# The last projection of a two-layer hybrid backbone: its sixteen row tiles inside the attention's pools

## The chip, the cores and the metric

The kernel runs on one core of a Trainium2 chip. The metric is the device time of one execution in microseconds (us). A core has a matrix engine (TensorE, PE in the profile), whose weight loads have a row of their own (PEld), and VectorE (DVE), ScalarE (ACT) and GpSimd (POOL). SyncE (SP) issues most of the DMAs; each engine takes its instructions in the order of its own queue.

## The reference, cut to what matters

Two layers run over 2048 latent tokens of width 1024 with 256 context tokens ahead of them. The second, odd layer is a neighbourhood attention with 16 heads of 64. Its end is all that the change touches:

```
def odd_mixer(h, hc, w_in, q_gain, k_gain, rpb, w_out, update_ctx):
    ...
    o = neighborhood_attention(q_x, k_x, v_x, k_c, v_c, rpb)
    y = jnp.dot(o.reshape(h.shape[0], h.shape[1], C_WIDTH) * jax.nn.silu(z_x), w_out)
    ...
x = x + gate * y
```

So for each block of 128 tokens (a row tile) the attention's output is multiplied by its gate path, then by a 1024 x 1024 weight, then by a gate vector, and added to the residual stream.

## The kernel before

**Numbers.** All values are float32. A product of matrices is made from two halves of each operand, a rounded high part and the remainder, in the type float32r: high by high, high by low, low by high, three matmuls for each slice of 128 in the sum (L129 to L131 in `mm3_steps`). One row tile of the projection is two halves of 512 columns by eight slices by three, 48 matmuls of 128 x 512.

**The attention.** `odd_attention` (L1306) goes over eight pairs of heads (j) and, in each, over twenty steps: four of context keys and sixteen blocks of 128 latent keys, n = 0 to 15. A step makes scores on TensorE (L1373, L1374), adds a table to them on VectorE (L1535), takes exp on ScalarE, and four to six steps later `flush` multiplies the result by the values (L1406) and adds it to running sums on GpSimd (L1412). For each block of 512 query tokens (bb = 0 to 3) `finish_block` divides by the sums (L838 to L845) and stores the result in a DRAM scratch RT1 from GpSimd's queue (L848). For the last pair the blocks are finished after n = 7, 11 and 15 (two at once).

**The tag "opt".** `exps` (L1322) hands out tiles of 4 KB a partition from a pool with eleven buffers of one tag. The exps of the attention live there, and so do the raw slices of the output weight (L1443), which is loaded and split in the last pair of heads while the attention still runs. The two halves of the weight go into buffers that the attention no longer needs (old query tiles, a value tile, tables, context keys).

**The end.** Row tile 0 is made ready inside the last steps: z0 (gate path) and r0 (attention's output) are loaded and multiplied (L1549 to L1551), x0 (residual) and the gate vector are loaded, and hi0 and lo0 are split (L1558); these are five tiles of "opt". After the last step z1, r1 and x1 of row tile 1 are loaded (L1564 to L1568; x1 in the place of the mask). Then come 6 triples of matmuls of tile 0, the rest of the attention (`flush(4)`), the rest of tile 0, the product r1 times z1 on GpSimd (L1579), the last `flush(0)`, the split of r1 (L1584, into the place of the running sums "oacc0"), and tile 1's matmuls.

**The separate stage.** `odd_attention` then closes the pools that it opened itself, and `odd_tail` (L1589) opens three new ones (wpA, wpS on chip, wpP in PSUM) and calls `project` for row tiles 2 to 15 (L1598). `project` (L1080) loads z, r and x of a tile (`project_load`, L1045), multiplies r by z on GpSimd (L1056), splits (`project_split`, L1059: high part on ScalarE, remainder on VectorE at L1061), and runs `project_steps` (L1063): 48 matmuls, after each 24 the gate on VectorE (L1072) and the residual on GpSimd (L1073), then the store of the tile from SP's queue (L1074). Every tag there has two buffers (four PSUM banks).

**Order of the work.** The program is traced as written; a planner then simulates it and puts every engine's queue in order, so that an instruction may be moved ahead of others whose inputs come later. Three things bind it: a tile's buffer has to be free, `issue_after` puts what is traced behind a named instruction of the same engine, and `load` (L108) chains the loads of the attention on SP's queue in the order of the text. The loads of `project_load` have no such chain.

Of the kernel before, what the change touches and what calls it, by code (L numbers as in the profile page):

```python
# [11 lines left out]
F32R = mybir.dt.float32r  # L12
AF = mybir.ActivationFunctionType
ALU = mybir.AluOpType
AX = mybir.AxisListType
PSUM = bass.MemoryType.PSUM

P = 128
D = 1024
KD = D // P  # L20
SEQ = 2048
CTX = 256
T = SEQ + CTX
NT = T // P
NCT = CTX // P
# [63 lines left out]
class Kern:  # L89
# [1216 lines left out]
    def odd_attention(self, out, right, left, wout):  # L1306

        nc = self.nc
        self.RT1 = self.scr("RT1", (KD, P, SEQ), F32)
        NR, NC = (len(b) for b in BLOCKS["k"])  # L1310
        with ExitStack() as es:
            self.ln_exp(self.last_tanh, es)
            kcp, vp, qa, qb, kp, tp, lp = right
            ap, rp, fp, ep = [self.pool(es, "oa" + n, bufs=2, side="left", reuse_waits="tile") for n in "KRFP"]
            pp = self.pool(es, "oaP", bufs=2, space=PSUM, reuse_waits="tile")
# [5 lines left out]
            bank = lambda: self.tl(pp, [P, 512], "st", bufs=4)  # L1321
            exps = lambda shape=[P, 2, 512], dt=F32: self.tl(ep, shape, "opt", dt, bufs=11)  # L1322
# [132 lines left out]
            def rows(tile, RT, o, ks):  # L1455
                self.load(tile[:, ks, :], RT[ks, :, o * P : o * P + P].rearrange("j p t -> p j t"))
# [15 lines left out]
            all_k, most_k = slice(0, KD), slice(0, KD - 1)  # L1472
# [18 lines left out]
            for j in range(8):  # L1491
                OA[j] = {}, {}
                for s, (kind, n) in enumerate(steps):
                    g, c = divmod(n, 4)
# [19 lines left out]
                    for i in range(2):  # L1514
# [17 lines left out]
                        for ro, ri, rn in pieces("k", 0, g, r0_, nr):  # L1532
                            for co, ci, cn in pieces("k", 1, c, c0, w):
                                d = slice(ro, ro + rn), slice(co, co + cn)
                                nc.vector.tensor_tensor(out=pt[:, d[0], d[1]], in0=ps[:, d[0], d[1]],  # L1535
                                                        in1=tabs[j][i][:, ri : ri + rn, ci : ci + cn], op=ALU.add)
# [15 lines left out]
                    elif j == 7 and n == 12:  # L1552
                        x0 = exps([P, D])
                        self.load(x0[:], self.x1[CTX : CTX + P, :])
                        gate = ones["kt"][0][:].rearrange("p i c -> p (i c)").bitcast(F32)
                        self.load(gate, self.gates[1, 0:1].partition_broadcast(P))
                        hi0, lo0 = [exps([P, KD, P], F32R) for _ in range(2)]
# [3 lines left out]
                            flush(4)  # L1561
            for _ in out_s:
                pass
            z1, r1 = [exps([P, KD, P]) for _ in range(2)]  # L1564
            rows(z1, self.z1, 1, all_k)
            rows(r1, self.RT1, 1, all_k)
            x1 = self.tl(ap, [P, NR, NC], "maskk", bufs=1)[:].rearrange("p r c -> p (r c)")[:, :D]
            self.load(x1, self.x1[CTX + P : CTX + 2 * P, :])  # L1568
            y = lambda: self.tl(fp, [P, 512], "rc", bufs=3)
            first = self.project_steps(hi0, lo0, x0, gate, wout, bank, y, out[:P, :])  # L1570
            with self.tc.issue_after(mm.ins):
                for _ in range(6):
                    mm = next(first)
# [2 lines left out]
            with self.tc.issue_after(mm.ins):  # L1576
                for mm in first:
                    pass
            nc.gpsimd.tensor_tensor(out=r1[:], in0=r1[:], in1=z1[:], op=ALU.mult)  # L1579
            with self.tc.issue_after(mm.ins):  # L1580
                flush(0)
            parts = self.tl(rp, [P, 2, 16, 64], "oacc0", F32R, bufs=1)
            hi1, lo1 = [parts[:, i].rearrange("p r c -> p (r c)").rearrange("p (k t) -> p k t", k=KD) for i in range(2)]
            self.project_split(r1[:], hi1, lo1)  # L1584
            for _ in self.project_steps(hi1, lo1, x1, gate, wout, bank, y, out[P : 2 * P, :]):
                pass
        return gate

    def odd_tail(self, out):  # L1589
        with ExitStack() as es:  # L1590
            kcp, va, qb0, vb, tb, lp, ta, qa, kp, qb1 = [self.pool(es, "oa" + n, bufs=2, side="right", reuse_waits="tile")
                                                         for n in ("KC", "VA", "QB", "VB", "TB", "L", "TA", "QA", "KT", "QC")]
            left = self.pool(es, "wpX", side="left", reuse_waits="tile")
            w = {}
            gate = self.odd_attention(out, (kcp, (va, vb), qa, (qb0, qb1), kp, (ta, tb), lp), left, w)
            ld, sp = [self.pool(es, n, bufs=2, side="left", reuse_waits="tile") for n in ("wpA", "wpS")]
            pp = self.pool(es, "wpP", bufs=2, space=PSUM, reuse_waits="tile")
            self.project(1, self.RT1, [(t, t - NCT) for t in range(NCT + 2, NT)], self.x1, out, w, sp, pp, ld, {}, [gate], self.z1)  # L1598

    def build(self, es, out):  # L1600
        self.consts(es)
# [95 lines left out]
```

## Time and profile before

| what | value |
|---|---|
| time, median of 3 runs | 3742.54 us (3739.37 to 3745.3) |
| the profiled execution's own time | 3737.21 us |
| span of its profile | 3735.4 us |
| TensorE busy | 3586.5 us, 96% of the span |
| VectorE, ScalarE, GpSimd busy | 2377.3, 1438.4, 1209.3 us |
| mean granted TensorE clock | 0.977 of full speed |

How to read it: the page's times are those of one profiled execution, counted from the start of its span. "PE pj L131" is a matmul of line 131 that writes a tile named pj. In brackets behind an instruction stands how long its engine was idle ahead of it and what ended that. In the table by stretches each engine has its busy time and, after x, its instructions; behind them come the granted clock of TensorE, the share of the DMA engines that was busy and the GB/s. Matmuls overlap: one of 128 x 512 is shown as 0.39 us, while the next starts 0.23 us after it.

### The profile page before, as it was taken

What the parts mean: (1) busy time and instruction counts of PE and PEld (TensorE: products, weight loads), DVE (VectorE), ACT (ScalarE), POOL (GpSimd) and SP (SyncE); (2) the same over time, 40 slices, a digit from 0 to 9 for tenths busy, and PEclk for the clock granted to TensorE, in tenths of its full rate; (3) what the DMA queues carried; (4) which work ended last, traced back from release to release, by engine and by line L of the source; (5) the groups of instructions that cost most, each with busy time, mean ns of one, the idle gap of its engine ahead of it and who ended that gap; (6) DMA issues with size and microseconds to landing.
All of it is one profiled execution on the core that took longest, in us unless ns stands there. A gap on an engine that the chain in (4) does not pass through costs nothing.

```text
span 3735.4 us, 51753 instructions
## 1 busy us (share of the span) xinstructions
PE 3586.5 (96%) x18404; PEld 2766.2 (74%) x18404; DVE 2377.3 (64%) x4860; ACT 1438.4 (39%) x2741; POOL 1209.3 (32%) x1336
## 2 busy tenths in 40 slices
PE   7999989999999999999999999999899999999889
PEld 6988987888886666655657878888688886555567
DVE  4677656888866666697654345545578774566722
ACT  4445541111125555545552134444322224444400
POOL 1434330001011222212202233333444435776643
PEclk9999999999999999999999999999999999999999
DMA  7455452222242241434515545445544438778464
GB/s 258 135 167 160 128 170 95 82 76 85 74 137 66 69 113 58 115 88 136 143 51 169 168 145 152 147 142 169 187 139 135 140 104 228 182 197 206 144 194 129
DMA packets 364371, 512.18 MB, mean 137 GB/s; under 512 B 25825, under 2 KB 243889, under 8 KB 358210
## 3 DMA queue, kind: packets, MB, share of 16 engines
q1 hardware_dynamic: 322642, 425.49, 39.1%
q0 software_dynamic: 19872, 55.92, 5.0%
q10 hardware_dynamic: 21600, 27.46, 2.1%
q8 instruction: 146, 2.39, 0.3%
q14 instruction: 111, 0.91, 0.1%
HBM read 329.38 MB, written 179.37 MB: 136 GB/s over the span
## 4 chain that ended last, share of the span: by engine, by line
PE 78%; DMA 9%; DVE 7%; ACT 2%; POOL 2%; issue 2%; SPq 0%; POOLq 0%; ACTq 0%; DVEq 0%
PE gm L129 9%; PE gm L130 9%; PE gm L131 9%; PE av L905 7%; PE st L963 4%; PE mx L651 4%; PE st L964 3%; PE st L965 3%; PE pj L129 3%; PE pj L130 3%; PE pj L131 3%; DMA kt<-K1t 2%; PE o L1406 2%; PE st L1373 2%; DMA wraw<-w_od 1%
## 5 line engine op out<-in xcount | busy, mean ns | idle before, releaser
L954 DVE TENSOR_TENSOR acc<-acc,apt 128x512 f32<-128x512 f32 x512 | 365.4, 738 | 155.9 <-ACT apt L106 153.0
L106 ACT ACTIVATE apt<-st 128x512 f32<-128x512 f32 (+1 forms) x592 | 344.6, 594 | 284.1 <-PE st L965 250.8
L652 DVE TENSOR_REDUCE mm<-mx 128x1 f32<-128x512 f32 (+1 forms) x656 | 389.2, 629 | 82.0 <-PE mx L651 75.0
L905 PE MATMUL av<-apt,av 128*64 128x512 f32 (+1 forms) x1184 | 287.6, 599 | 0.0
L963 PE MATMUL st<-aq,akh 97*128 97x512 f32 (+1 forms) x592 | 254.0, 429 | 5.1 <-ACT apt L106 2.7
L651 PE MATMUL mx<-mk,mq 96*128 96x512 f32 (+1 forms) x656 | 236.7, 373 | 6.3 <-DMA mq<-QT 4.7
L964 PE MATMUL st<-aq,akh 96*128 96x512 f32 (+1 forms) x592 | 235.3, 398 | 0.0
L965 PE MATMUL st<-aq,akl 96*128 96x512 f32 (+1 forms) x592 | 234.1, 396 | 0.0
L1286 DVE CUSTOM_DVE_ANT_1 mx<-mx,mtab 128x225 f32<-128x225 f32 (+12 forms) x576 | 183.8, 339 | 59.5 <-PE mx L1280 44.2
L1535 DVE TENSOR_TENSOR opt<-st,tab 128x64 f32<-128x64 f32 (+10 forms) x576 | 143.0, 316 | 115.5 <-PE st L1374 90.2
L106 ACT ACTIVATE u<-gm 128x352 f32<-128x352 f32 (+1 forms) x140 | 68.6, 497 | 371.0 <-PE gm L131 208.7
L905 PEld LDWEIGHTS av<-apt,av 128*64 128x64 f32 x1184 | 82.0, 138 | 156.8 <-issue 155.5
L963 PEld LDWEIGHTS st<-aq,akh 97*128 97x128 f32 x592 | 112.3, 190 | 98.0 <-issue 43.7
L1412 POOL TENSOR_TENSOR oacc<-oacc,opt 128x682 f32<-128x682 f32 (+9 forms) x144 | 169.5, 1200 | 28.0 <-ACT opt L106 26.9
L1073 POOL TENSOR_TENSOR px<-py,px 128x512 f32<-128x512 f32 x64 | 86.4, 1350 | 232.2 <-DVE py L1072 229.6
L106 ACT ACTIVATE opt<-opt 128x930 f32<-128x930 f32 (+8 forms) x130 | 104.4, 805 | 123.9 <-DVE opt L1535 115.1
L106 ACT ACTIVATE prh<-pr 128x1024 fp32r<-128x1024 f32 x32 | 33.9, 1058 | 263.0 <-PE pj L130 235.3
L651 PEld LDWEIGHTS mx<-mk,mq 96*128 96x128 f32 x656 | 121.7, 189 | 17.8 <-issue 5.1
L1373 PE MATMUL st<-q,kt 128*128 128x480 f32 (+5 forms) x256 | 104.4, 410 | 31.6 <-DVE opt L1535 15.9
L965 PEld LDWEIGHTS st<-aq,akl 96*128 96x128 f32 x592 | 113.7, 192 | 25.5
L964 PEld LDWEIGHTS st<-aq,akh 96*128 96x128 f32 x592 | 114.0, 193 | 18.1
L106 ACT ACTIVATE x<-px,modB,modA 128x128 f32<-128x128 f32 x272 | 99.3, 469 | 58.0 <-PE px L331 55.3
(517 smaller groups left out, 10097.4 us busy)
## 6 DMA issues: line engine op xcount, KB each, us to landing
q<-Q SPq DMA_DIRECT2D x48, 512.0 KB
H<-x ACTq DMA_DIRECT2D x36, 512.0 KB
adaw<-ada_w SPq DMA_DIRECT2D x64, 256.0 KB
x<-H SPq DMA_DIRECT2D x32, 512.0 KB
pr<-RT SPq DMA_DIRECT2D x32, 512.0 KB
wraw<-w_od SPq DMA_DIRECT2D x64, 256.0 KB
K1t<-okt POOLq DMA_DIRECT2D x32, 512.0 KB, 7.7
kt<-K1t SPq DMA_DIRECT2D x32, 512.0 KB
```

The source lines that it names most:

```text
L106: return self.nc.scalar.activation(out, in_, func, **kw)
L129: self.nc.tensor.matmul(out, lh(k), rh(k), start=j == 0, stop=False)
L130: self.nc.tensor.matmul(out, lh(k), rl(k), start=False, stop=False)
L131: yield self.nc.tensor.matmul(out, ll(k), rh(k), start=False, stop=j == n - 1)
L651: mm = nc.tensor.matmul(ps[:, :w], q[:A_QK, (t % 6) * P : (t % 6) * P + P], k[:A_QK, k0 : k0 + w], start=True, stop=True)
L652: nc.vector.tensor_reduce(out=m[:, t, n : n + 1], in_=ps[:, :w], axis=AX.X, op=ALU.max)
L905: nc.tensor.matmul(O[j, nb][i * 64 : i * 64 + 64, :w], V[j, kt // TT][:, kt % TT, i * 64 : i * 64 + 64], pts[i][:, :w], start=n == 0, stop ...
L954: nc.vector.tensor_tensor(out=acc[i][:, :w], in0=a[:, :w], in1=pts[i][:, :w], op=ALU.add)
L963: nc.tensor.matmul(ps[:, :w], kh[: A_QK + 1, i, kq], qh[: A_QK + 1, :w], start=True, stop=False)
L964: nc.tensor.matmul(ps[:, :w], kh[:A_QK, i, kq], ql[:A_QK, :w], start=False, stop=False)
L965: mm = nc.tensor.matmul(ps[:, :w], kl[:A_QK, i, kq], qh[:A_QK, :w], start=False, stop=True)
L1286: nc.vector.tensor_tensor_reduce(out=s, in0=s, in1=tb[:, ri : ri + rn, ci : ci + cn], scale=1.0, scalar=-3e38, op0=ALU.add, op1=ALU.max, a ...
```

## The change

The stage of `project` and its three pools are gone; `odd_tail` now only calls `odd_attention`, and all sixteen row tiles run in that function's pools. `fetch(o)` takes three tiles of "opt" and loads z, r and x of row tile o through the chained `load`; `ready` multiplies r by z on GpSimd, takes two more tiles of "opt" (five for each row tile; tile 1 keeps "oacc0" for its halves) and splits. Tiles 1 and 2 are fetched ahead of tile 0's matmuls. In the loop, ahead of the matmuls of tile o, tile o + 1 is made ready and tile o + 2 is fetched. x1 is no longer in the mask's place. The product of tile 1 now stands behind the last `flush(0)` in the text. PSUM banks are the attention's tag "st" (four) in place of "pj" (four), and the tiles between VectorE and GpSimd are its tag "rc" (three) in place of "py" (two). `project_steps`, `project_split` and `load` are unchanged.

```diff
-            z1, r1 = [exps([P, KD, P]) for _ in range(2)]
-            rows(z1, self.z1, 1, all_k)
-            rows(r1, self.RT1, 1, all_k)
-            x1 = self.tl(ap, [P, NR, NC], "maskk", bufs=1)[:].rearrange("p r c -> p (r c)")[:, :D]
-            self.load(x1, self.x1[CTX + P : CTX + 2 * P, :])
             y = lambda: self.tl(fp, [P, 512], "rc", bufs=3)
-            first = self.project_steps(hi0, lo0, x0, gate, wout, bank, y, out[:P, :])
+            tok = lambda o: slice(CTX + o * P, CTX + o * P + P)
+
+            def fetch(o):
+                z, r, x = exps([P, KD, P]), exps([P, KD, P]), exps([P, D])
+                rows(z, self.z1, o, all_k)
+                rows(r, self.RT1, o, all_k)
+                self.load(x[:], self.x1[tok(o), :])
+                return z, r, x
+
+            def ready(z, r, x, parts=None):
+                nc.gpsimd.tensor_tensor(out=r[:], in0=r[:], in1=z[:], op=ALU.mult)
+                hi, lo = parts or [exps([P, KD, P], F32R) for _ in range(2)]
+                self.project_split(r[:], hi[:], lo[:])
+                return hi, lo, x
+
+            steps_of = lambda o, hi, lo, x: self.project_steps(hi, lo, x, gate, wout, bank, y, out[o * P : o * P + P, :])
+            first = steps_of(0, hi0, lo0, x0)
+            got = {o: fetch(o) for o in (1, 2)}
             with self.tc.issue_after(mm.ins):
                 for _ in range(6):
                     mm = next(first)
...
-            nc.gpsimd.tensor_tensor(out=r1[:], in0=r1[:], in1=z1[:], op=ALU.mult)
             with self.tc.issue_after(mm.ins):
                 flush(0)
             parts = self.tl(rp, [P, 2, 16, 64], "oacc0", F32R, bufs=1)
...
-            self.project_split(r1[:], hi1, lo1)
-            for _ in self.project_steps(hi1, lo1, x1, gate, wout, bank, y, out[P : 2 * P, :]):
-                pass
-        return gate
+            got[1] = ready(*got[1], parts)
+            for o in range(1, NT - NCT):
+                if o + 1 < NT - NCT:
+                    nxt = ready(*got.pop(o + 1))
+                if o + 2 < NT - NCT:
+                    got[o + 2] = fetch(o + 2)
+                for _ in steps_of(o, *got.pop(o)):
+                    pass
+                got[o + 1] = nxt
 
     def odd_tail(self, out):
...
-            w = {}
-            gate = self.odd_attention(out, (kcp, (va, vb), qa, (qb0, qb1), kp, (ta, tb), lp), left, w)
-            ld, sp = [self.pool(es, n, bufs=2, side="left", reuse_waits="tile") for n in ("wpA", "wpS")]
-            pp = self.pool(es, "wpP", bufs=2, space=PSUM, reuse_waits="tile")
-            self.project(1, self.RT1, [(t, t - NCT) for t in range(NCT + 2, NT)], self.x1, out, w, sp, pp, ld, {}, [gate], self.z1)
+            self.odd_attention(out, (kcp, (va, vb), qa, (qb0, qb1), kp, (ta, tb), lp), left, {})
```

More of the change, by code (lines that the diff above doesn't have):

```diff
@@ L1582, in odd_attention @@
             parts = self.tl(rp, [P, 2, 16, 64], "oacc0", F32R, bufs=1)
-            hi1, lo1 = [parts[:, i].rearrange("p r c -> p (r c)").rearrange("p (k t) -> p k t", k=KD) for i in range(2)]
-            self.project_split(r1[:], hi1, lo1)
-            for _ in self.project_steps(hi1, lo1, x1, gate, wout, bank, y, out[P : 2 * P, :]):
-                pass
-        return gate
+            parts = [parts[:, i].rearrange("p r c -> p (r c)").rearrange("p (k t) -> p k t", k=KD) for i in range(2)]
+            got[1] = ready(*got[1], parts)
[7 more added lines that the diff above has]
+                got[o + 1] = nxt
     def odd_tail(self, out):
```

## The prediction, made before the changed kernel was run

> **What bounds the kernel now.** I read the page's strip of forty slices first, then a table by stretches around the place that the change touches, then the instructions of TensorE there in order of time, and last the chain of work that ended last between the two stages.
>
> ```profile
> PE   7999989999999999999999999999899999999889
> PEclk9999999999999999999999999999999999999999
> ```
>
> TensorE is busy almost everywhere, so only time in which it is idle or slow can be won. The next table is cut at the seam between the attention's function and the separate stage (start:end, length, then busy time of PE, PEld, DVE, ACT and POOL with instructions, granted clock, DMA share, GB/s).
>
> ```profile
> 3518.00:3525.40 7.40, 2.18 (x9) 1.57 (x9) 5.31 (x12) 3.15 (x5) 4.35 (x4) 0.76 0.22 70
> ...
> 3554.50:3567.60 13.10, 0.24 (x2) 0.00 (x0) 0.71 (x2) 1.06 (x1) 3.60 (x2) 0.69 0.86 228
> 3567.60:3581.30 13.70, 13.70 (x48) 10.94 (x49) 3.13 (x3) 1.06 (x1) 9.26 (x4) 0.80 0.87 242
> 3581.30:3592.50 11.20, 11.20 (x50) 9.02 (x49) 3.61 (x3) 1.06 (x1) 5.08 (x4) 1.00 0.61 188
> 3592.50:3715.30 122.80, 122.80 (x529) 99.02 (x528) 40.67 (x33) 11.66 (x11) 49.77 (x31) 1.00 0.53 167
> ```
>
> Three things are to be seen. In the stage itself (the last row) TensorE is busy for 122.80 of 122.80 us at full clock: nothing can be won or hidden there. At the seam it is idle for a whole 13 us. And the first tile behind the seam, 48 matmuls, takes 13.70 us at a granted clock of 0.80, where the next takes 11.20 at 1.00. The seam itself, by instruction:
>
> ```profile
> 3554.35 0.40 PE L131 MATMUL st<-kc,oacc 128*128 128x512 f32 x1
> 3567.60 0.79 PE L129 MATMUL pj<-wo,prh 128*128 128x512 f32 x1 [12.86 <-ACT prh L106]
> 3568.20 0.63 PE L130 MATMUL pj<-wo,prh 128*128 128x512 f32 x1
> ...
> 3581.32 0.39 PE L129 MATMUL pj<-wo,prh 128*128 128x512 f32 x1
> ```
>
> And why it is there, from the chain that ended last (start, length, what):
>
> ```profile
> 3554.78 0.70 DVE rc L1072
> ...
> 3555.55 1.27 POOL maskk L1073
> ...
> 3556.84 0.34 SPq L1074
> ...
> 3557.71 6.25 DMA pr<-RT
> ...
> 3564.12 2.35 POOL pr L1056
> ...
> 3566.50 1.06 ACT prh L106
> ```
>
> Tile 1's last matmul, its gate, its residual and its store run first; only behind that store does SP's queue issue the loads of tile 2, in the new pools. Then 6.25 us of transfer, 2.35 us of product, 1.06 us of split. Nothing of tile 2 was begun ahead of the seam.
>
> **The change part by part.** *The seam goes.* If tile 2 is ready when tile 1's matmuls end, the next matmul follows at the stage's pace. The last one of tile 1 starts at 3554.35 and the pace is 11.17 us a tile (below), 0.23 a matmul, so tile 2 starts at 3554.58 and not at 3567.60: 13.02 us.
>
> ```profile
> 3583.61 0.35 SPq L1074 DMA_DIRECT2D out_dram<-px  x1
> ...
> 3706.52 0.34 SPq L1074 DMA_DIRECT2D out_dram<-px  x1
> ```
>
> The pace: these are the stores of tiles 2 and 13, eleven tiles apart, (3706.52 - 3583.61) / 11 = 11.17.
>
> *The slow restart goes with it.* From the first matmul of tile 2 to the first of tile 3 are 3581.32 - 3567.60 = 13.72 us; at the pace it would be 11.17. That is 2.55 us. Sum of both: 15.57 us.
>
> The Trainium skill, "TensorE: Matmul & The Clock Gate", section "What's actually happening", says that an idle TensorE falls to half clock and that about 3.4 us of sustained work release it. By that page alone the restart would cost half of 3.4, 1.7 us, and the sum would be 14.7, an estimate from the page. The trace agrees on the mechanism (0.69 and 0.80 granted around the gap), and has 2.55 us for the size.
>
> *Is tile 2 ready by 3554.58?* Its five tiles need buffers of "opt". When tile 1 is fetched, the eleven are all taken: z0, r0, x0, hi0, lo0, two raw weight slices, and the exps of n = 12 to 15. They come free as follows (rows by engine in order of time: SP's queue, VectorE, TensorE, GpSimd; start, length).
>
> ```profile
> 3522.80 0.37 SPq L111 DMA_DIRECT2D opt<-z  x1
> 3525.90 0.37 SPq L111 DMA_DIRECT2D opt<-RT  x1
> 3526.32 0.57 SPq L111 DMA_DIRECT2D maskk<-x  x1
> ```
> ```profile
> 3523.66 2.02 DVE L1535 TENSOR_TENSOR opt<-st,tab 128x248 f32<-128x248 f32 x8
> ...
> 3527.71 3.73 DVE L1061 TENSOR_TENSOR kc<-opt,kc 128x512 fp32r<-128x512 f32 x2
> ```
> ```profile
> 3531.20 2.28 PE L1406 MATMUL o<-opt,ov 128*64 128x72 f32 x32
> ```
> ```profile
> 3541.55 0.69 DVE L1072 TENSOR_TENSOR rc<-st,kt 128x512 f32<-128x512 f32 x1 [1.70 <-PE st L131]
> ...
> 3547.23 0.69 DVE L845 TENSOR_TENSOR rc<-o,rc 128x512 f32<-128x512 f32 x1
> ```
> ```profile
> 3543.31 0.50 PE L129 MATMUL st<-wo,oacc 128*128 128x512 f32 x1
> ```
> ```profile
> 3530.86 2.82 POOL L1579 TENSOR_TENSOR opt<-opt,opt 128x1024 f32<-128x1024 f32 x1
> 3536.73 2.21 POOL L1073 TENSOR_TENSOR opt<-rc,opt 128x512 f32<-128x512 f32 x1 [3.06 <-DVE rc L1072]
> 3540.15 0.56 POOL L848 DMA_DIRECT2D RT<-rc  x1 [1.20 <-DVE rc L845]
> 3542.33 1.27 POOL L1073 TENSOR_TENSOR opt<-rc,opt 128x512 f32<-128x512 f32 x1 [1.62 <-DVE rc L1072]
> ```
>
> z1 and r1 take the places of z0 and r0 as now. x1 and z2 take those of the raw slices, the later of which is free when its split ends, 3531.44. The other four are free when the last 32 value matmuls end, 3533.48: r2, x2, hi2, lo2. So r2 is issued near 3534. At the seam's transfer of 6.25 us, the dearest near row, it lands by 3540.2. GpSimd then has a store to issue and a residual until 3543.60; if the product waits behind both, it ends 2.82 us later, at 3546.4, and the split's high part 1.06 us after that, 3547.5. The remainder on VectorE costs 2152 ns (next fence) and may stand behind the last blocks' division, which ends at 3547.9: 3550.1. That is 4.5 us early even with everything against it. The cover is tile 0's and tile 1's matmuls, from 3525 to 3554; should it fall short, every us beyond 4.5 comes back as idle time of TensorE.
>
> *Steady tiles.* Loads, product, split, gate, residual and store are the same instructions in the same number as in the stage, whose groups are these (busy us, mean ns):
>
> ```profile
> L1073 POOL TENSOR_TENSOR px<-py,px 128x512 f32<-128x512 f32 x28 | 36.2, 1292 | 87.3 <-DVE py L1072 87.3
> L1056 POOL TENSOR_TENSOR pr<-pr,pz 128x1024 f32<-128x1024 f32 x14 | 34.5, 2465 | 14.3 <-DMA pr<-RT 12.9 <-issue 1.5
> L1061 DVE TENSOR_TENSOR prl<-pr,prh 128x1024 fp32r<-128x1024 f32 x14 | 30.1, 2152 | 17.3 <-ACT prh L106 15.8
> L1072 DVE TENSOR_TENSOR py<-pj,kt 128x512 f32<-128x512 f32 x28 | 19.4, 692 | 105.2 <-PE pj L131 105.2
> L106 ACT ACTIVATE prh<-pr 128x1024 fp32r<-128x1024 f32 x14 | 14.8, 1060 | 145.4 <-PE pj L130 120.4 <-POOL pr L1056 25.0
> ```
>
> Per tile of 11.17 us GpSimd has 2465 + 2 x 1292 = 5.0 us and VectorE 2152 + 2 x 692 = 3.5: both have room. ScalarE's wait "<-PE pj L130 120.4" says that with two buffers the split of a tile starts when the matmuls two tiles back let go of theirs, and TensorE still waits for nothing. Eleven shared buffers must do the same: while tile o runs it holds hi, lo, x; tile o - 1 holds x until its store has landed; tile o + 1 holds z, r, x, hi, lo. That is nine, and z and r of tile o + 2 make eleven. It fits, and z and r of o + 1 come free in the middle. I cost it at nothing.
>
> *Queues.* The six added loads stand in a chain on SP's queue. Behind a load that waits for a buffer stand only later loads and stores, no work of TensorE. The product of tile 2 can hold up GpSimd's stores of RT1 (2.82 us); the first tile that reads a late one is tile 4, due at 3554.58 + 2 x 11.17 = 3576.9, far off. The split of tile 2 on VectorE can stand ahead of a bank's release: at most 2.15 us, and of the four banks the one tile 1's second half takes is free 6.7 us ahead of need (gate of tile 0 done at 3542.2, need at 3548.9, from tile 1's start at 3543.31 and half a tile). Nothing, with 2.15 us as the end of the bound.
>
> *Moved order.* New work in reach of the planner can shift the attention's last steps, which I can't bound but by the first row of the table: of 7.40 us there, TensorE is idle for 5.2. A better order could win up to that, a worse one lose as much and more (second rival).
>
> **Sum.** 3737.21 - 15.57 = 3721.6 against the profiled execution's own time (span 3735.4 to 3719.8). The median of the runs is 5.33 us above that execution; on the median's level the forecast is 3742.54 - 15.57 = **3727.0 us**.
>
> **The rivals.** *Bubbles between tiles (slower).* Eleven buffers are shared, and a fetched tile may take the buffers that hi and lo of the next tile need. Then hi and lo get theirs only when the running tile's own come free, at its end. Each of the 13 boundaries from tile 2 on would show the split: 1.06 on ScalarE, then 2.15 on VectorE, less the two matmuls that need no remainder (0.47): 2.74 us, in all 35.6, and 20.0 slower net: 3762.6. With the remainder at the 1.23 us that the seam's tiles show where GpSimd is quiet, 1.82 x 13 = 23.7, net 8.1 slower: 3750.7. It decides against the change from 15.57 / 13 = 1.20 us a boundary.
>
> ```profile
> 3567.58 1.23 DVE L1061 TENSOR_TENSOR prl<-pr,prh 128x1024 fp32r<-128x1024 f32 x1 [12.11 <-ACT prh L106]
> ```
>
> For it: the count above is exactly eleven. Against it: hi and lo of o + 1 stand ahead of the fetch in the text, and two sets were enough in the stage. The Trainium skill speaks for looking here: "Perfetto Trace Analysis", section "Optimization Strategy", says that the same gap coming back on the engine that should be full can mean too little memory for the next tile. The stage before shows no such gap.
>
> *The fetches hold up the attention.* Four more buffers are asked for while n = 14 and 15 still want theirs. If a fetch takes one first, the table's addition at 3523.66 waits for the last raw slice, until 3531.44: 7.8 us, which TensorE can't fill, and 7.8 are left of the gain: 3734.8. Against it: now z1 waits for z0's own place although the exps of n = 11 are done with, which looks as if places were kept for the earlier text.
>
> *The seam stays.* The planner could place tile 2's loads behind tile 1's store on SP's queue as now; the change then does not do what it says: 3742.5. Against it: the chain puts them directly behind x1, which goes out at 3526.32.
>
> **How the numbers follow.** Forecast 0.66; attention held up 0.12; seam stays 0.08; bubbles 0.14. The range begins at 3720, the forecast less the 5.2 us that a better order could give and some of the runs' own spread (3 us to each side), and reaches over the second rival to 3740; the bubbles and most of the case without a change are left out. A measurement of this kernel can tell about 0.2% (7.5 us) from no change. The second rival lies at that bound and is split in half: faster 0.66 + 0.06 = 0.72, same 0.06 + 0.08 = 0.14, slower 0.14.
>
> **What would show it.** In the changed kernel's profile tile 2's first matmul follows tile 1's last without idle time, near 3554.6 of the span; the granted clock stays at 1.00 from there; stores stay 11.17 us apart; GpSimd's first product of a steady tile ends before 3550. Idle time of TensorE ahead of each tile's first matmul, "<-ACT" or "<-DVE", would be the first rival; matmuls of n = 14 and 15 later than now the second. The forecast is wrong if the last attention matmul moves by more than a few us, or if the pace of the tiles isn't 11.17.

## The result and the profile after

| | before | changed |
|---|---|---|
| median of 6 runs each | 3746.07 us (3739.37 to 3747.4) | 3729.07 us (3725.5 to 3732.9) |
| profiled execution, span | 3735.4 us | 3729.0 us (its own time 3730.79) |
| from tile 0's first matmul to the end of the span | 3735.4 - 3525.36 = 210.04 us | 3729.0 - 3534.94 = 194.06 us |

The ratio is 0.9958 with a 95% interval of 0.9945 to 0.9971: 0.42% faster, some 15.7 us (the two medians are 17.0 us apart). A second measurement of the same changed kernel gave 0.9955 [0.9942, 0.9968].

The two spans differ by only 6.4 us, and the third row of the table says why. Up to tile 0's matmuls the instructions stand in the same order on all five engines in both kernels, yet the changed kernel's execution arrives there 9.58 us later. Other profiled executions below arrive anywhere between 3521 and 3546; the latest of them is the kernel before with nothing altered ahead of tile 1's end ("Idle time without the slow clock"). The profiled execution of before (3737.21 us) was also faster than all six timed runs of that kernel, the one of the changed kernel slower than its median. What lies ahead of tile 0 is therefore left out of every comparison of two traces here, and they are compared from that matmul on. The difference is then 210.04 - 194.06 = **15.98 us**; the prediction's sum was 15.57.

The page's strip of the changed kernel:

```profile
PE   7999989999999999999999999999899999988899
```

The eights now lie in the attention; the last two slices, the row tiles, are nines. The table by stretches, with the columns that the prediction gives, cut at the first matmuls of tiles 2 and 3:

```profile
3553.00:3564.00 11.00, 11.00 (x48) 8.86 (x48) 6.27 (x10) 2.37 (x4) 6.63 (x6) 1.00 0.67 205
3564.00:3575.16 11.16, 11.16 (x49) 9.01 (x48) 2.52 (x3) 1.06 (x1) 4.96 (x3) 1.00 0.65 220
3575.16:3700.00 124.84, 124.84 (x538) 100.81 (x537) 25.25 (x31) 10.62 (x10) 49.49 (x30) 1.00 0.54 166
```

Before had 13.10 us with 0.24 busy ahead of tile 2 and then 13.70 us for its 48 matmuls. Now tile 1 (first row, 11.00 of 11.00 us busy) runs straight into tile 2 (second row, 11.16 of 11.16), both at full clock. The same in TensorE's instructions in order of time, from the last waits of the attention on:

```profile
3530.44 0.40 PE L1373 MATMUL st<-q,kt 128*128 128x352 f32 x1 [2.37 <-DVE rc L844]
3533.85 0.59 PE L1373 MATMUL st<-q,kt 128*128 128x264 f32 x1 [2.85 <-DVE opt L1535]
3534.94 0.74 PE L129 MATMUL st<-wo,opt 128*128 128x512 f32 x1
...
3563.78 0.39 PE L131 MATMUL st<-kc,oacc 128*128 128x512 f32 x1
3564.00 0.39 PE L129 MATMUL st<-wo,opt 128*128 128x512 f32 x1
...
3575.16 0.39 PE L129 MATMUL st<-wo,opt 128*128 128x512 f32 x1
```

and the same place of before:

```profile
3520.86 0.40 PE L1373 MATMUL st<-q,kt 128*128 128x352 f32 x1 [2.38 <-DVE rc L844]
3524.27 0.59 PE L1373 MATMUL st<-q,kt 128*128 128x264 f32 x1 [2.84 <-DVE opt L1535]
3525.36 0.73 PE L129 MATMUL st<-wo,opt 128*128 128x512 f32 x1
```

The waits of n = 14 and 15 are what they were (2.37 and 2.85 against 2.38 and 2.84). Tile 2 follows tile 1's last matmul after 0.22 us, with no idle time noted. How tile 2 became ready (SP's queue, GpSimd, ScalarE, VectorE):

```profile
3541.48 0.57 SPq L111 DMA_DIRECT2D opt<-RT  x1
...
3546.79 2.68 POOL L1575 TENSOR_TENSOR opt<-opt,opt 128x1024 f32<-128x1024 f32 x1 [3.53 <-DMA opt<-RT]
...
3549.51 1.06 ACT L106 ACTIVATE opt<-opt 128x1024 fp32r<-128x1024 f32 x1 [3.63 <-POOL opt L1575]
...
3550.60 1.23 DVE L1061 TENSOR_TENSOR opt<-opt,opt 128x1024 fp32r<-128x1024 f32 x1 [2.78 <-ACT opt L106]
```

It is ready at 3550.60 + 1.23 = 3551.83 and needed at 3564.00: 12.2 us early.

One thing is not as foretold. These are stores and loads on SP's queue and two operations of GpSimd between them, in the steady part of the changed kernel:

```profile
3656.13 0.35 SPq L1074 DMA_DIRECT2D out_dram<-opt  x1
...
3660.77 0.37 SPq L111 DMA_DIRECT2D opt<-RT  x1
...
3664.77 2.40 POOL L1575 TENSOR_TENSOR opt<-opt,opt 128x1024 f32<-128x1024 f32 x1 [5.54 <-DMA opt<-RT]
3667.12 1.30 POOL L1073 TENSOR_TENSOR opt<-rc,opt 128x512 f32<-128x512 f32 x1
3667.19 0.33 SPq L111 DMA_DIRECT2D opt<-x  x1
3668.45 0.35 SPq L1074 DMA_DIRECT2D out_dram<-opt  x1
```

The stores are 12.32 us apart and not 11.17, although TensorE goes on at 11.16 a tile. Read from top to bottom this is a loop: a store goes out; 4.64 us later an r load; 4.00 us after that the product; behind it on GpSimd the residual of an older tile, and on SP's queue an x load, both as the product ends; and 0.03 us after that residual's end the next store. TensorE does not feel it in this execution. Two of the experiments ask whether it is a loop, and whether it would be felt.

### The profile page after: what moved, and what is told of

Read it like the earlier page. It is cut to its first block, busy times and chain, and to the rows that moved or that the text cites. A ratio compares the mean times of both kernels' runs of the same rounds, so it can differ in the third digit from the quotient of the medians.

```text
span 3729.0 us, 51761 instructions
## 1 busy us (share of the span) xinstructions
PE 3588.5 (96%) x18404; PEld 2769.4 (74%) x18404; DVE 2361.5 (63%) x4860; ACT 1437.8 (39%) x2741; POOL 1207.5 (32%) x1336
## 4 chain that ended last, share of the span: by engine, by line
PE 79%; DMA 9%; DVE 5%; POOL 2%; ACT 2%; issue 2%; SPq 0%; POOLq 0%; ACTq 0%; DVEq 0%
PE gm L129 9%; PE gm L130 9%; PE gm L131 9%; PE av L905 7%; PE st L963 4%; PE mx L651 4%; PE st L964 3%; PE st L965 3%; DMA kt<-K1t 3%; PE pj L129 2%; PE pj L131 2%; PE pj L130 2%; PE o L1406 2%; PE st L129 2%; PE st L131 2%
## 5 line engine op out<-in xcount | busy, mean ns | idle before, releaser
L106 ACT ACTIVATE opt<-opt 128x930 f32<-128x930 f32 (+9 forms) x144 | 119.2, 829 | 269.0 <-POOL opt L1575 138.6
L1373 PEld LDWEIGHTS st<-q,kt 128*128 128x128 f32 x256 | 53.1, 208 | 85.6 <-issue 50.5
L129 PE MATMUL gm<-w0h,hhi 128*128 128x512 f32 x288 | 115.7, 402 | 0.0
```

What stands on the lines that cost most here:

```text
L106: return self.nc.scalar.activation(out, in_, func, **kw)
L129: self.nc.tensor.matmul(out, lh(k), rh(k), start=j == 0, stop=False)
```

## The experiments

The theory: the gain is the order of the loads on SP's queue and nothing else. Tile 2 is prepared while tiles 0 and 1 run, so the idle time and the slow tile behind it go. Rivals: the closed stage itself costs the time (its pools, its banks); the room in "opt" is just enough and would turn into bubbles; time was won or lost in the attention's end. Where a difference in us is worked out from a ratio, it is that ratio's distance from 1 times the median of before in the same measurement. Lines that name an engine, a line and what it waited for (PE st L129 <- ...) give the us waited in total, how often, and the longest.

**Order of the loads alone.** Pools, banks and buffers as changed; only tile 2's loads are chained behind tile 1's store (its product and split then follow tile 1's matmuls in the text too).

```diff
-            got = {o: fetch(o) for o in (1, 2)}
+            got = {1: fetch(1)}
...
+                if o == 1:
+                    for _ in steps_of(o, *got.pop(o)):
+                        pass
+                    self.chain = self.store
+                    got[2] = fetch(2)
...
```

> The changed kernel with one thing put back: on SP's queue the loads of row tile 2 stand behind the store of row tile 1, as in the kernel before; pools, buffers and everything else stay as changed. My theory (the gain is the seam that those late loads open, 13.0 us, and the slow restart behind it, 2.55 us): the gap of TensorE in front of tile 2 is back, 12 to 14 us, tile 2 takes 13 to 14 us instead of 11.2, and the time is that of the kernel before, ratio 0.999 to 1.001. First rival (the gain comes from giving up the separate pools, or from another order in the last attention steps): the ratio stays near 0.996 although the loads are late.

Measured: 3746.7 us, ratio 0.9992 [0.9983, 1.0001]; from tile 0 to the end 209.34 us against 210.04 of before. TensorE in order of time:

```profile
3564.50 0.40 PE L131 MATMUL st<-kc,oacc 128*128 128x512 f32 x1
...
3577.15 0.79 PE L129 MATMUL st<-wo,opt 128*128 128x512 f32 x1 [12.25 <-ACT opt L106]
...
3591.11 0.39 PE L129 MATMUL st<-wo,opt 128*128 128x512 f32 x1
```

Tile 2 was due at 3564.73 and comes 12.42 us late; it then takes 13.96 us, 2.80 over the pace. Together 15.2 us: the whole gain is gone with the pools still merged. The closed stage as such costs nothing that can be measured.

**The seam one tile later.** Tiles 0 to 2 inside, the old separate stage from tile 3 on.

```diff
-            for o in range(1, NT - NCT):
+            for o in (1, 2):
...
+            self.project(1, self.RT1, [(t, t - NCT) for t in range(NCT + 3, NT)], self.x1, out, w, sp, pp, ld, {}, [gate], self.z1)
```

> Tiles 0 to 2 run as in the changed kernel, the separate stage with its pools does tiles 3 to 15 as before. My theory (the seam costs what it costs wherever it lies, because the stage's first loads are issued only behind the last inner tile): the gap of 12 to 14 us moves behind tile 2, tile 3 takes 13 to 14 us, ratio to the kernel before 0.999 to 1.001. Rival (each tile run inside gains something, about 1.1 us of the 15.6 for each of fourteen): 0.9997 and no gap of that size. Second rival (early loads of tile 2 are enough): 0.996.

Measured: 3746.79 us, ratio 0.9995 [0.9986, 1.0003]; from tile 0 to the end 210.78 us.

```profile
3570.43 0.40 PE L131 MATMUL st<-kc,opt 128*128 128x512 f32 x1
...
3583.70 0.80 PE L129 MATMUL pj<-wo,prh 128*128 128x512 f32 x1 [12.86 <-ACT prh L106]
...
3597.40 0.39 PE L129 MATMUL pj<-wo,prh 128*128 128x512 f32 x1
```

The idle time has moved to the new seam, 3583.70 - 3570.66 = 13.04 us, and the slow tile with it, 13.70 - 11.16 = 2.54. The sum is 15.58, the prediction's 15.57 at another place. Tile 2, now inside, shows neither.

**Idle time without the slow clock.** Before, with 52 filler matmuls behind tile 1 into a bank that nobody reads, so that TensorE works through all of the seam but its last 1.21 us.

```diff
+            with self.tc.issue_after(mm.ins):
+                fill = self.tl(pp, [P, 512], "o", bufs=4)
+                for k in range(52):
...
+                    nc.tensor.matmul(fill[:], a[:, :P], b, start=k == 0, stop=k == 51)
```

> The kernel before, with 52 more matmuls of 128 x 512 on TensorE behind tile 1's (into a PSUM bank that nobody reads), to keep it busy while tile 2 is loaded. They add work to the seam and nothing to the result. My theory (2.55 us of the gain are a slow restart after idle time): tile 2 still starts 13 us after tile 1's end, but its 48 matmuls take 11.2 us and not 13.7, at a granted clock of 1.00; the time falls by about 2.5 us, ratio 0.9993. Rival (tile 2 is slow for another reason, such as its remainder coming late from VectorE or six loads at once): it still takes 13 to 14 us.

Measured: 3747.19 us, ratio 0.9995 [0.9985, 1.0004]: too small for the time to tell. The trace tells it, tile 2's first and tile 3's first matmul:

```profile
3588.62 0.50 PE L129 MATMUL pj<-wo,prh 128*128 128x512 f32 x1 [1.21 <-ACT prh L106]
...
3600.21 0.39 PE L129 MATMUL pj<-wo,prh 128*128 128x512 f32 x1
```

Tile 2 takes 11.59 us in place of 13.72, at a granted clock of 1.00 in place of 0.80. So keeping TensorE busy is worth 2.13 of the restart's 2.55 us. The 0.42 that is left is for the most part a wait of the first L131 for its remainder, 0.25 us; in before the slow matmuls covered that wait, and nearly all of the 2.55 us lies in the first 13 matmuls, 3567.60 to 3572.90, at a granted clock of 0.50. The Trainium skill, "TensorE: Matmul & The Clock Gate", section "What's actually happening", has an idle TensorE fall to half clock. The trace agrees on that; the prediction's estimate from this page, 1.7 us, took 3.4 us at half clock, and here it lasted 5.30.

**How early must the loads be?** The changed kernel with tile o + 1 fetched only behind the store of tile o - 1: one tile ahead, not two.

```diff
+                    self.chain = last
+                    got[o + 1] = fetch(o + 1)
...
-                if o + 2 < NT - NCT:
-                    got[o + 2] = fetch(o + 2)
...
+                last = self.store
```

> The changed kernel with less distance: the loads of tile o + 1 stand behind the store of tile o - 1 on SP's queue, so they go out some 2.5 us after tile o's matmuls begin; all else as changed. My theory (the chain of a tile, about 2.5 us of transfer, 2.4 to 2.8 of product, 1.06 and 1.23 to 2.15 of split, fits under the 11.17 us of the tile before, so that one tile ahead just does): TensorE does not wait, stores stay 11.17 us apart, ratio 0.995 to 0.997. Rival (two tiles ahead are needed): a wait of 1 us or more in front of each tile's first matmul, 13 to 20 us in all, ratio 0.999 to 1.002.

Measured: 3757.71 us, ratio 1.0024 [1.0014, 1.0035], slower than before; from tile 0 to the end 3755.6 - 3534.49 = 221.1 us. My expectation failed. TensorE's waits in the row tiles, then a stretch of the chain that ended last:

```profile
PE st L129 <- ACT opt L106: 13.5, 8, 2.5
PE st L131 <- DVE opt L1061: 3.1, 5, 0.9
```
```profile
3592.83 0.35 SPq L1074
...
3593.76 5.85 DMA opt<-RT
...
3599.77 2.40 POOL opt L1575
...
3602.20 1.06 ACT opt L106
...
3603.28 1.70 DVE opt L1061
```

I had put the r transfer too low: it takes 5.85 us here, next to z and x of the same tile. From the store to the end of the high part are 3603.26 - 3592.83 = 10.4 us, to the end of the remainder 12.15, and the store itself comes some time after its tile. That is more than one tile of 11.16 us leaves. The wait comes ahead of every other tile, eight of the fourteen. The distance of two tiles is not a luxury: with one, the change would have been a loss.

**How much room does "opt" need?** The changed kernel with two, four or six of the eleven buffers held from tile 2 on, so that nine, seven or five are left.

```diff
+                if o == 2:
+                    hold = [exps([P, D]) for _ in range(6)]
+                    for t in hold:
+                        nc.gpsimd.memset(t[:, :1], 0.0)
...
```

> The changed kernel in which, from row tile 2 on, two of the eleven buffers of the tag opt are held by tiles that do nothing (a memset of one column at the start, an addition of one column at the very end); nine are left. My theory (nine hold the running tile's hi, lo, x, the last tile's x, and z, r, x, hi, lo of the next; loads for the tile after that start when the split frees z and r): TensorE does not wait in the tiles, ratio to the kernel before 0.995 to 0.997. Rival (eleven was just enough, so that each buffer less makes bubbles between tiles): waits of TensorE of 1.8 to 2.7 us at each of 13 boundaries, ratio 1.002 to 1.006.

> The same with four of the eleven held, seven left. My theory, with the length of the chain that the run with just-in-time loads showed (r lands 5.5 to 5.9 us after its issue, product 2.4, split 1.06 and 1.2 to 1.8): z and r of the tile after next find no room until the running tile ends, so the chain begins about with the tile and takes 10.5 to 12 us of its 11.17: right at the edge, waits of 0 to 1.5 us at every or every other boundary, ratio 0.996 to 1.001. Rival (the count of buffers decides nothing as long as one tile fits): 0.9958 with no wait.

> The changed kernel with six of the eleven opt buffers held from tile 2 on, so that five are left; the output is the reference's. Theory (bubbles need fewer buffers than the tile in work and its successor hold): hi, lo and x of the running tile and z and r of the next fill the five; the high part of the next can take z's place, but its remainder finds a place only when the running tile lets go of one, at its end. Each boundary from tile 3 on then shows the remainder, 1.2 to 2.2 us, less the 0.47 of matmuls that need none: 0.8 to 1.7 us a tile, 10 to 22 us in all, 3742 to 3755 us, with TensorE waiting <-DVE opt L1061 in every tile. Rival (the slack of the loads decides, not the place of the halves): the loads of a tile go out only when the tile before is split, the product comes late, and TensorE waits <-ACT opt L106 for 3 us and more a tile: over 3770 us. Should there be no wait in the tiles at all, 3731 us, the buffers are no limit at any number that can be built.

Measured: nine 3734.47 us, 0.9959 [0.9946, 0.9972]; seven 3735.11, 0.9963 [0.9951, 0.9976]; five 3766.19, 1.0057 [1.004, 1.0074]. With nine TensorE waits nowhere in the tiles; with seven once, for 0.2 us; the waits at every or every other boundary that I had expected with seven did not come. With five, in the row tiles:

```profile
PE st L131 <- DVE opt L1061: 14.7, 13, 1.1
PE st L129 <- ACT opt L106: 12.5, 13, 1.0
```

Thirteen boundaries, each with a wait for the high part and one for the remainder: these are the bubbles of the first rival. A steady boundary costs 2.64 us: stores go out at 3590.82 and 3604.62, 13.80 apart, less 11.16. The rival had 2.74 us and a net loss of 20.0; the run is 0.0057 x 3745.38 = 21.3 us slower than before. The terms are the rival's too: 1.06 us of high part and 2.3 of remainder, less the matmuls that need no remainder, of which there are four here and not two. My own expectation for this run was too low, since it gave the high part a place in z's buffer; in fact both halves wait for the running tile's end (ScalarE <-PE st L130, VectorE behind it). So the rival's price was right and its condition was not: it begins between seven and five buffers, not at eleven.

**Is the loop of store and load a loop, and would it be felt?** The changed kernel, with tiles 2 to 15 worked a second time, once with eleven buffers and once with nine.

```diff
+            row = lambda o: o if o < NT - NCT else o - 14
...
-            for o in range(1, NT - NCT):
+            for o in range(1, NT - NCT + 14):
```

> The changed kernel with its loop run over 14 tiles more (tiles 2 to 15 a second time, the same values written again), eleven buffers. Without any wait this is 14 x 11.16 = 156.2 us more than the changed kernel: 3887 to 3888 us. Theory (the loop of store, load, product and next store takes 12.3 to 12.8 us with eleven buffers, TensorE needs 11.16 a tile, and only the cushion of the first tiles hides it): in the changed kernel the cushion is used up at tile 15, so the second pass pays 1.2 to 1.6 us a tile, 17 to 22 us: 3904 to 3910 us, with TensorE waiting <-DVE rc L1072 or <-ACT opt L106 at most boundaries of the second half, and stores still 12.3 to 12.8 us apart. Rival (the loop only uses slack that is there and goes faster once TensorE is waiting for it): 3888 us within 3, stores 11.2 us apart in the second pass.

> The same 14 tiles more, with two of the eleven buffers held from tile 2 on. Theory (with nine buffers the planner puts a tile's x load ahead of the store before it, and the loop keeps 11.16 us a tile): 3888 us within 3, no wait of TensorE in the tiles, stores 11.16 us apart to the end, so 15 to 20 us faster than with eleven buffers. Rival (the drift has nothing to do with the order that eleven buffers lead to): the same time as with eleven, within 0.1%.

Measured: eleven buffers 3903.63 us, 1.0421 [1.04, 1.0442]; nine 3887.47 us, 1.038 [1.0365, 1.0396]. More room is slower by 16.2 us in the medians (I had 17 to 22); from tile 0 to the end 3889.8 - 3521.45 = 368.35 against 3885.0 - 3534.60 = 350.40, 17.95 us. TensorE's waits in the tiles with eleven, and the first of them:

```profile
PE st L129 <- DVE rc L1072: 14.7, 14, 1.7
```
```profile
3707.95 0.46 PE L129 MATMUL st<-wo,opt 128*128 128x512 f32 x1 [1.08 <-DVE rc L1072]
```

Fourteen waits, none before tile 16, the first of the second pass (tile 2 starts at 3550.46; fourteen tiles of 11.16 later it is 3706.7), and then one a tile. With nine there is none. In one turn of this loop late in the eleven-buffer run the chain that ended last reads:

```profile
3843.34 4.44 DMA out_dram<-opt
...
3847.85 4.31 DMA opt<-RT
...
3852.37 2.41 POOL opt L1576
...
3854.80 1.24 DMA opt<-x
```

The store has to land before the r load gets its buffer, and the load has to land for the product. The next store then waits for two things that stand behind the product: a residual on GpSimd (1.30 us, from 3854.73), and on SP's queue the x load that the chain names. Together 4.4 + 4.3 + 2.4 + 1.3 = 12.4 us a turn. That is 1.2 us more than TensorE needs for a tile.

With nine buffers the order is another one, on SP's queue and on GpSimd (the kernel of sixteen tiles, one engine after the other):

```profile
3644.89 0.37 SPq L111 DMA_DIRECT2D opt<-z  x1
3645.98 0.37 SPq L111 DMA_DIRECT2D opt<-RT  x1
3647.95 0.35 SPq L1074 DMA_DIRECT2D out_dram<-opt  x1
3651.67 0.33 SPq L111 DMA_DIRECT2D opt<-x  x1
...
3659.11 0.35 SPq L1074 DMA_DIRECT2D out_dram<-opt  x1
```
```profile
3646.63 1.29 POOL L1073 TENSOR_TENSOR opt<-rc,opt 128x512 f32<-128x512 f32 x1 [2.95 <-DVE rc L1072]
3650.56 2.40 POOL L1575 TENSOR_TENSOR opt<-opt,opt 128x1024 f32<-128x1024 f32 x1 [2.64 <-DMA opt<-RT]
```

Here the load that waits for the store to land is x (3.3 us), which no product needs. The r load goes out ahead of the store, and the residual for which the store waits runs ahead of the product. So the loop is open, and the stores are 11.16 us apart. My expectation for the long run with nine buffers, whose queue has this same order, held in the time and had the order the wrong way round: with nine buffers the x load stands behind the store, with eleven ahead of it.

The changed kernel lives on the cushion of 12 us that tile 2 had, that is, on the time by which tile 2 was ready early; it lasts for about as many tiles as there are. In its second measurement two boundaries near the end already wait, for 0.44 and 1.25 us. At sixteen tiles nine and eleven buffers still take the same time (0.9959 and 0.9955 in one measurement).

**Another order at the attention's end.** The product of tile 0 goes ahead of eight running sums on GpSimd, to shorten the wait of n = 15.

```diff
+                        prod = nc.gpsimd.tensor_tensor(out=r0[:, most_k, :], in0=r0[:, most_k, :], in1=z0[:, most_k, :], op=ALU.mult)
...
+                                late_sums.enter_context(self.tc.issue_after(prod.ins))
```

> The changed kernel with one product moved on GpSimd: r0 times z0 of row tile 0 goes ahead of the eight running sums of the last pair's third block, behind which it stands now. In the changed kernel's profile the steps n = 14 and 15 wait for it: TensorE idles 2.4 and 2.85 us and then runs some nine matmuls at half pace. My theory: the wait of 2.85 us falls to about 1 us and part of the slow restart goes, 2 to 4 us in all, ratio to the kernel before 0.9948 to 0.9953, to the changed one 0.9990 to 0.9995. Rival (the sums are delayed by the product's 2.1 us and the next wait, for the sums or for a bank, takes its place): no difference from the changed kernel.

> The changed kernel itself again, on the same chip as the three others of this call, so that they can be compared with it. Expected: ratio to the kernel before 0.9945 to 0.9971 as measured, and a start of row tile 0's matmuls that differs from the first profile by several us, because that profile had lost some 9.5 us ahead of all that the change touches.

Measured, beside each other: 3731.8 us, 0.9955 [0.9938, 0.9971], and the changed kernel again 3733.25, 0.9955 [0.9942, 0.9968]. TensorE's waits from 3490 on, with the moved product:

```profile
PE st L1373 <- DVE rc L844: 5.0, 1, 5.0
...
PE st L129 <- DVE rc L844: 2.0, 1, 2.0
```

My expectation failed and the rival held. The 2.85 us of n = 15 have shrunk to 0.19, but 2.37 have become 5.0, and a new wait of 2.0 stands ahead of tile 1: waits that change places. This end was not won by moving this one instruction. The changed kernel's second profile reaches tile 0 at 3533.82, only 1.1 us from the first and not the several us that I had expected.

## Why the prediction was right, and where its reasons were not

- **The seam goes (13.02 us).** Shown: 0.22 us from matmul to matmul, and the order of tile 2's loads alone, in the merged pools, brings 12.42 us back.
- **The slow restart (2.55 us).** Shown: tile 2 at 11.16 us; with the loads put back, 2.80. It is the clock: 13 matmuls at half clock make nearly all of it in before. Keeping the clock up there wins 2.13 and not 2.55 us, because the late remainder is then waited for.
- **Sum 15.57 us, forecast 3727.0 us.** 15.98 us between the traces, 15.7 by the ratio, 3729.07 us measured. The two medians of before (3742.54, 3746.07) differ by more than the forecast is off, so that the level was met within 2.1 us is in part luck. The same sum on the profiled execution (3721.6) missed by 9.2 us, about what that execution had lost ahead of tile 0.
- **Is tile 2 ready?** Yes, and 12.2 us early instead of 4.5. The r load went out 6.5 us after tile 0's first matmul, where I had 8.6; the transfer was within the 6.25 us that I took; GpSimd's product did not stand behind the store and the residual, and the remainder took 1.23 us and did not stand behind the division. I had taken all of these at their worst.
- **Steady tiles at nothing.** Right in time, wrong in reason. "Stores stay 11.17 us apart" failed: they are 12.3 us apart. The step that failed is the one on the queues, "Behind a load that waits for a buffer stand only later loads and stores, no work of TensorE". The stores are what frees buffers, so a load that waits for a store, with the next store behind the product that waits for that load, closes a loop. I had counted buffers (eleven) and each engine's work in a tile (5.0 and 3.5 us), and had not added up the time once round. It cost nothing in the first profile, and waits of 1.7 us in the second, only because there are sixteen tiles.
- **Queues and the attention's end at nothing.** Right: the waits of n = 14 and 15 are unchanged. Read by the clock of the span, the prediction's sign for its second rival (n = 14 and 15 later than now) came up, by 9.6 us; but these us are lost ahead of the waits, and the ratio, 15.7 us, agrees with the stretch from tile 0 on.
- **Rivals.** Bubbles: not at eleven, nine or seven buffers, and at the foretold price with five. The lower price of 1.82 us rests on a misreading: GpSimd was not quiet at the seam, a product had begun there at 3567.70, after the remainder (see the last section). Fetches that hold up the attention: refuted by the unchanged waits. The seam stays: did not happen; built as an experiment, it gives the time of before.

Open: which semaphores the planner set so that the x load goes ahead of the store with eleven buffers and behind it with nine was not taken apart; shown is only that the order differs, and the time with it. No run changes that order alone and leaves the eleven buffers. The 9.58 us by which the two traces differ ahead of tile 0 were left out, not explained.

## What to carry to other kernels

If a matrix engine is idle between two stages, look at when the next stage's first loads are issued; what counts is their place in the queue, and they have to be out by the whole chain of load, product and split ahead of need, here 10 to 12 us or one tile and more. When loads and stores share buffers and a queue, add up one turn (store, load, what works on it, and what the next store waits for) and compare it with the time of a tile: each engine may have room and the loop still be too long. A loop that is too long shows first in the distance of the stores, and as waits of the busy engine only when the cushion is gone; and more buffers are not always the safer choice, if, as here, another order of the queues comes with them.

## What was not expected of the hardware

**VectorE and GpSimd hold each other up, and the one that begins second pays.** Of before, VectorE's remainder and then GpSimd at the same moment:

```profile
3649.42 2.31 DVE L1061 TENSOR_TENSOR prl<-pr,prh 128x1024 fp32r<-128x1024 f32 x1
...
3649.36 1.30 POOL L1073 TENSOR_TENSOR px<-py,px 128x512 f32<-128x512 f32 x1 [1.93 <-DVE py L1072]
```

Of the kernel with nine buffers, where GpSimd does nothing from 3654.2 to 3657.8:

```profile
3655.89 1.22 DVE L1061 TENSOR_TENSOR opt<-opt,opt 128x1024 fp32r<-128x1024 f32 x1 [4.71 <-PE st L130]
```

The same subtraction takes 1.22 us alone and 2.31 beside a residual on GpSimd that began 0.06 us earlier and is not slowed itself (1.30 us in either). The means agree: 2315 ns for nine of them in before, 1225 ns for nine in this kernel. Where the remainder begins first, it is the other way round; of before, at tile 1:

```profile
3536.57 1.22 DVE L1061 TENSOR_TENSOR oacc<-opt,oacc 128x1024 fp32r<-128x1024 f32 x1
...
3536.73 2.21 POOL L1073 TENSOR_TENSOR opt<-rc,opt 128x512 f32<-128x512 f32 x1 [3.06 <-DVE rc L1072]
```

The remainder keeps its 1.22 us, and the residual takes 2.21. The product that begins at 3567.70, 0.12 us after a remainder, takes 3.34 us in place of 2.40. Wherever the two overlap by more than 0.2 us in the traces of this case, the one that began second is the longer. The Trainium skill, "GPSIMD Engine Reference", section "1. Specifications", has GpSimd and VectorE share their interface to SBUF, with contention for operations of VectorE with two SBUF inputs; both pairs above agree with it.

**A transfer has no one duration.** The r load of 512 KB took 4.0 us from issue to product in the steady changed kernel, where it goes out alone, and 5.85 us beside z and x of its tile; the seam of before had 6.25. What a load costs was read best from the row whose neighbours in the queue are the same.
